# A hybrid decoder step on one core: block transpositions within SBUF, a new layout of two scratch tensors, and the first modulation's weights in tiles of 256 columns

## The chip, the cores and the metric

The kernel runs on one core of a Trainium2 chip. Its metric is device time in microseconds, as the median of several runs. The work is spread over five instruction streams: TensorE (PE, with its weight loads as PEld), VectorE (DVE), ScalarE (ACT), GpSimd (POOL) and SyncE (SP), whose queue issues every DMA of this kernel.

## What is computed

One step of a decoder with two layers, for a prompt of 1024 tokens and 8 samples of one token, which share the weights. Cut from the reference:

```python
cs = jax.nn.silu(c)
for layer in range(DEPTH):                       # 2
    mod = cs @ ada_w[layer] + ada_b[layer]       # (1024 x 3072) weights
    shift, scale, gate = jnp.split(mod[:, None, :], 3, axis=-1)
    h = _rms(x, norm_w[layer]) * (1.0 + scale) + shift
    # layer 0: gated DeltaNet heads (8) and mLSTM heads (8)
    # layer 1: GLA heads (4) and retention heads (4)
    y, states = mixer(h, ...)                    # h @ w_in, the heads, silu gate, @ w_out
    x = x + gate * y
return _rms(x, final_norm_w), states
```

The chunked gated delta rule solves, for each head and each chunk of 128 tokens, a unit lower triangular system `(A + I) U = rhs`.

## The kernel before

**Activations** stand with channels in the partitions and the 1032 tokens (1024 of the prompt, 8 samples) along the free side. Input and output projections are TensorE matmuls in which each factor is split into a high and a low half; weights come in tiles of 512 KB, 1024 rows by 128 columns, are split by ScalarE and VectorE (`halves`), and one projection of 128 columns is 72 matmuls of 344 tokens.

**The order** of all instructions is not that of the program text. The class `Recorder` collects every operation with what it reads and writes (`add`, `touch`), estimates its cost, and plans forward and backward passes over all of them; then `emit` writes each engine's instructions in the planned order. So all instructions of the trace have the line of `emit`, L448, and groups are told apart by tiles. For a DMA, the planner counts 0.36 us on SP's queue, then 0.45 us, its bytes by a rate that follows the shortest run, and 1.4 us to landing, or 2.1 us over 256 KB. For a scratch tensor in DRAM, `region` takes the range from the first to the last element of an access as what it touches, and two accesses whose ranges overlap, one of them a write, are planned one after the other. SP carries out its list in order: a DMA that waits holds up those behind it. Every engine is in order in that sense.

**The start.** `program` loads x, turns it (`turn_x`), takes the root mean squares by token (`rms_tokens`), and normalizes x into eight tiles `xr` (s_aT, s_Y, s_mq, s_mk, s_va, s_kwe, s_qs, s_mp in the trace). Then four groups g follow. In each, `ada_first` (L665) loads four tiles of the first modulation's weights (shift and scale, 2 x 2 blocks of 128 columns with all 1024 rows), multiplies them with the conditioning vectors `cT`, and sums four row groups of TensorE; `layer_h0` makes two of the eight channel blocks of h, and the gates' and the first projection's matmuls for these blocks follow. In the trace the tiles are the loads from in_ada_w before 50 us, and their matmuls those into bank B.

**`squares`** (L1697) turns channels into tokens. VectorE transposes blocks of 32 x 32 from x to y; then the blocks, grouped by 32 partitions, have to change places between partition groups. This is done by DMA: y is written to one of four scratch tensors td in DRAM, 128 rows of 4 KB, and read back in four transfers of 32 partitions, each with four runs of 1 KB per partition. The result is a view of z. Callers are `gdn_mix` (k into s_N, v into s_v; two for each of 8 heads), `mlstm_pair_mix` (s_qs; 4 pairs), `mlstm_mix` (s_pt), `mlstm_out` (s_mp; 8 heads each) and `v_tokens` (s_u, s_v; two for each GLA and each retention head). The written tiles are s_kd, s_vs, s_kwe and s_va.

**`inverse`** (L1279) inverts the triangular system of one gated-delta head. Its diagonal blocks of 32 x 32, for 8 chunks and 4 blocks, are written to the scratch tensor nd in four DMAs, one for each block j, with runs of 128 B. They are read back as 64 blocks of 16 x 16 (`by16`), inverted by 15 steps on VectorE in s_EM, written to the scratch tensor yd and read back by blocks j. The 64 rows of nd and yd are ordered `(c j q)`: chunk, block, half of the block, so that the four blocks j interleave.

In the page, the tensor yd of the output projection's inputs has the same name as the scratch tensor yd of `inverse`; s_EM tells the latter.

Of the kernel before, what the change touches and what calls it, by code (L numbers as in the profile page):

```python
# [9 lines left out]
F32 = mybir.dt.float32  # L10
# [7 lines left out]
T = 1024  # L18
# [4 lines left out]
KT = 8  # L23
L = 128
NC = T // L
# [438 lines left out]
class Step:  # L464
# [200 lines left out]
    def ada_first(self, g, load):  # L665

        nc, a, V = self.nc, self.a, self.nc.vector
        acc = self.ps("B")
        for x in range(4):
            w = load().rearrange("p (k c) -> p k c", k=KT)  # L670
            c0 = 1024 * (x // 2) + 128 * (2 * g + x % 2)
            with self.urgent():
                nc.sync.dma_start(w, a["ada_w"][0, :, c0:c0 + 128].rearrange("(k p) c -> p k c", p=128))
                for k in range(KT):
                    j = k % 4
                    self.mm(acc[32 * j:32 * j + 32, 128 * x:128 * x + 128], self.cT[:, k, :], w[:, k, :],
                            start=k < 4, stop=k >= 4, tile_position=(0, 32 * j))
        with self.urgent():
            sb = self.slot("qg", name="adasb")
            self.act(sb[:, 0:512], acc, AF.Copy)  # L680
            pt = self.ps("B")
            for x in range(4):
                self.tr(pt[:, 128 * x:128 * x + 128], sb[:, 128 * x:128 * x + 128])
            red = sb[:, 512:548].rearrange("p (x c) -> p x c", x=4)
            V.tensor_reduce(red, pt.rearrange("p (x j c) -> p x c j", x=4, j=4)[:, :, 0:9, :], axis=AX.X, op=ALU.add)
            k = slice(2 * g, 2 * g + 2)
            out = self.mod[0][:, 0:16].rearrange("p (s k) c -> p s k c", s=2)[:, :, k]
            o = self.vo["ada_b"]
            bias = self.vec[:, o:o + 16].rearrange("p (s k) -> p s k", s=2)[:, :, k]
            V.tensor_tensor(out, red.rearrange("p (s k) c -> p s k c", s=2),  # L690
                            bias.unsqueeze(3).to_broadcast([128, 2, 2, 9]), op=ALU.add)
            n = self.vo["norm_w"] + 2 * g
            V.scalar_tensor_tensor(self.am[0][:, k], out[:, 1], 1.0,
                                   self.vec[:, n:n + 2].unsqueeze(2).to_broadcast([128, 2, 9]),
                                   op0=ALU.add, op1=ALU.mult)
# [583 lines left out]
    def inverse(self, N):  # L1279

        V, G, dma = self.nc.vector, self.nc.gpsimd, self.nc.sync.dma_start

        nd, yd = (self.nyd[x][self.turn(x, 2)] for x in ("nd", "yd"))
        by32 = lambda x, j: x.rearrange("(c j q) x -> c j (q x)", c=NC, j=4)[:, j, 0:1024].rearrange(
            "c (s t) -> s c t", t=32)
        by16 = lambda x: x[:, 0:512].rearrange("m (r t) -> m r t", t=32)[:, :, 0:16]
        blocks = [slice(32 * j, 32 * j + 32) for j in range(4)]
        t = self.slot("EM", name="inv")
        D, At, qt, Dt = (t[:, 256 * i:256 * i + 256].rearrange("p (c t) -> p c t", c=NC) for i in range(4))
        nb, yb, tb = (t[0:64, 256 * i:256 * i + 256].rearrange("p (r t) -> p r t", t=16) for i in (1, 2, 3))  # L1290
        dma(yb, self.a["i16"].rearrange("p (r t) -> p r t", t=16))
        for j, b in enumerate(blocks):
            dma(by32(nd, j), N[b, :, b])
        dma(nb, by16(nd))
        for s in range(15):
            n = 15 - s
            V.tensor_tensor(tb[:, 0:s + 1, 0:n], yb[:, 0:s + 1, s:s + 1].to_broadcast([64, s + 1, n]),
                            nb[:, s:s + 1, s + 1:16].to_broadcast([64, s + 1, n]), op=ALU.mult)
            V.tensor_tensor(yb[:, 0:s + 1, s + 1:16], yb[:, 0:s + 1, s + 1:16], tb[:, 0:s + 1, 0:n], op=ALU.subtract)
        dma(by16(yd), yb)  # L1300

        for j, b in enumerate(blocks):
            dma(D[b], by32(yd, j))
        V.transpose(Dt, D)
        p = self.ps(None, [128, NC, 32])
        for c in range(NC):
            for j, b in enumerate(blocks):
                self.mm(p[b, c, :], N[b, c, b], Dt[b, c, :], tile_position=(32 * j, 32 * j))
        V.tensor_tensor(At, p, self.imask.unsqueeze(1).to_broadcast([128, NC, 32]), op=ALU.mult)
        p = self.ps(None, [128, NC, 32])  # L1310
        for c in range(NC):
            for j, b in enumerate(blocks):
                self.mm(p[b, c, :], At[b, c, :], D[b, c, :], tile_position=(32 * j, 32 * j))
        V.tensor_tensor(D, D, p, op=ALU.subtract)
        V.transpose(Dt, D)
        Y = self.slot("Y", [128, NC, L], name="Y")
        G.memset(Y, 0.0)
        for b in blocks:
            V.tensor_copy(Y[b, :, b], D[b])

        p = self.ps(None, [128, 2, NC, 32])
        for c in range(NC):
            for i in (0, 2):
                j = i + 1
                bi, bj = slice(32 * i, 32 * i + 32), slice(32 * j, 32 * j + 32)
                self.mm(p[bj, 0, c, :], N[bi, c, bj], Dt[bi, c, :], tile_position=(32 * i, 32 * j))
        for j in (1, 3):
            bj = slice(32 * j, 32 * j + 32)
            self.act(qt[bj], p[bj, 0], AF.Copy, scale=-1.0)
        p2 = self.ps(None, [128, NC, 64])  # L1330
        for c in range(NC):
            for i in (0, 2):
                j = i + 1
                bi, bj = slice(32 * i, 32 * i + 32), slice(32 * j, 32 * j + 32)
                self.mm(p2[bi, c, 0:32], qt[bj, c, :], D[bj, c, :], tile_position=(32 * j, 32 * i))
            self.mm(p2[32:64, c, 0:32], D[32:64, c, :], qt[32:64, c, :], tile_position=(32, 32))
        V.tensor_copy(Y[0:32, :, 32:64], p2[0:32, :, 0:32])
        V.tensor_copy(Y[64:96, :, 96:128], p2[64:96, :, 0:32])

        iy = t[:, 0:512].rearrange("p (c t) -> p c t", c=NC)  # L1340
        Yt = iy[0:64]
        G.memset(Yt[0:32, :, 32:64], 0.0)
        G.tensor_copy(Yt[0:32, :, 0:32], Dt[0:32])
        G.tensor_copy(Yt[32:64, :, 32:64], Dt[32:64])
        V.tensor_copy(Yt[32:64, :, 0:32], p2[32:64, :, 0:32])
        p3 = self.ps(None, [128, NC, 64])
        for c in range(NC):
            self.mm(p3[64:128, c, :], N[0:64, c, 64:128], Yt[:, c, :], tile_position=(0, 64))
        q3 = iy
        self.act(q3[64:128], p3[64:128], AF.Copy, scale=-1.0)  # L1350
        p4 = self.ps(None, [128, NC, 64])
        for c in range(NC):
            self.mm(p4[0:64, c, :], q3[64:128, c, :], Y[64:128, c, 64:128], tile_position=(64, 0))
        V.tensor_copy(Y[0:64, :, 64:128], p4[0:64])
        return Y
# [341 lines left out]
    def squares(self, y, x, z):  # L1697


        dma = self.nc.sync.dma_start  # L1700
        y, z = y[:, 0:T], z[:, 0:T]
        self.nc.vector.transpose(y.rearrange("p (b c j) -> p b c j", b=4, c=NC),
                                 x[:, 0:T].rearrange("p (c b i) -> p b c i", b=4, c=NC))
        d = self.td[self.turn("td", 4)]
        dma(d, y)
        for b in range(4):
            dma(z[32 * b:32 * b + 32].rearrange("i (a x) -> i a x", a=4),
                d.rearrange("(a i) (b x) -> b i a x", a=4, b=4)[b])
        return z.rearrange("p (a c j) -> p c a j", a=4, c=NC)

    def v_tokens(self, v):
# [407 lines left out]
    def build(self):  # L2119
        tc, nc = self.tc, self.nc  # L2120
        with ExitStack() as ctx:
            cp = ctx.enter_context(tc.tile_pool(name="cp", bufs=1))
            psum = ctx.enter_context(tc.tile_pool(name="psum", bufs=1, space=PSUM))
            dr = ctx.enter_context(tc.tile_pool(name="dr", bufs=1, space=DRAM))
# [17 lines left out]
            self.sd = [dr.tile([16, 128], F32, name=f"sd{i}") for i in range(2)]  # L2142
            self.spd = dr.tile([16, W], F32, name="spd")
            self.rd = [dr.tile([4, QB], F32, name=f"rd{i}") for i in range(2)]
            self.td = [dr.tile([128, T], F32, name=f"td{i}") for i in range(4)]
            self.nyd = {x: [dr.tile([64, 528], F32, name=f"{x}{i}") for i in range(2)] for x in ("nd", "yd")}
            self.program()
            with tc.manual_schedule():
# [104 lines left out]
```

## Time and profile before

| | us |
|---|---|
| median of 3 runs | 2255.21 |
| lowest, highest | 2254.8, 2257.08 |
| the profiled execution, its own time | 2262.98 |
| the profiled execution, its span | 2261.2 |
| granted TensorE clock, mean | 0.983 |

The span runs from the first to the last instruction. In the page's second part the span is cut into 40 slices of 56.5 us, with the busy share of each engine in tenths, and the DMA engines' below:

```profile
PE   6999999999999998998989999999999999999998
DVE  6775656576565756666553355745754754755322
DMA  9465564625172535527383222254253253365212
```

TensorE is busy nearly throughout but for the first slice; a busy PE is not PE at its peak. The start lasts to about 100 us, the even layer's heads to about 1195 us; its output projection, the odd layer and the last projection take the rest. In the timeline each row has its start and its length in us, the engine (SPq for the DMAs that SP issues), the operation, what is written and what is read, the count, and in brackets the engine's idle time before it and what ended it.

### The profile page before, as it was taken

Reading aid. Unit: us, or ns where it says so; the run is one execution under the profiler, and the core shown is the slowest. Engines: PE = TensorE matmul, PEld = TensorE weight load, DVE = VectorE, ACT = ScalarE, POOL = GpSimd, SP = SyncE. Lnnn points to the kernel's source line nnn. Section 1 sums busy time; section 2 is a strip of 40 time slices with the busy share of each in tenths; the row PEclk is TensorE's granted clock in tenths of the full one; section 3 lists DMA queues with packets and bytes.
Section 4 is the critical chain, followed back from the end, with each engine's and each line's share of the span. In section 5 each row is a group of like instructions: output and inputs, shape, how many; then the busy total and the mean of one; then the engine's idle time right before and its main releaser. Section 6 shows DMA issues by size and latency. Waiting matters only on the chain.

```text
span 2261.2 us, 42497 instructions
## 1 busy us (share of the span) xinstructions
PE 2184.1 (97%) x17532; PEld 2036.4 (90%) x17532; DVE 1312.8 (58%) x2559; ACT 761.4 (34%) x1374; POOL 588.4 (26%) x409
## 2 busy tenths in 40 slices
PE   6999999999999998998989999999999999999998
PEld 4877877999999988998889999999999999999997
DVE  6775656576565756666553355745754754755322
ACT  4432313242323323232341135234335334334322
POOL 3120212121121311202330032623622622634210
PEclk9999989999999999999999999999999999999999
DMA  9465564625172535527383222254253253365212
GB/s 263 134 190 161 138 190 115 177 78 149 48 189 75 160 99 123 137 77 189 100 253 117 74 80 69 73 153 124 76 157 119 76 162 106 110 192 176 81 59 92
DMA packets 323383, 290.61 MB, mean 129 GB/s; under 512 B 51963, under 2 KB 289013, under 8 KB 323182
## 3 DMA queue, kind: packets, MB, share of 16 engines
q1 hardware_dynamic: 323190, 287.91, 45.2%
q8 instruction: 137, 2.24, 0.4%
q14 instruction: 56, 0.46, 0.1%
HBM read 213.61 MB, written 74.44 MB: 127 GB/s over the span
## 4 chain that ended last, share of the span: by engine, by line
PE 81%; DMA 8%; DVE 6%; ACT 2%; issue 2%; SPq 1%; POOL 0%; POOLq 0%; ACTq 0%; DVEq 0%
PE pj L448 63%; PE A L448 12%; PE B L448 5%; SPq L448 1%; DMA wf<-in_ada_w 1%; DMA s_mp<-td 1%; DVE s_pt L448 1%; DVE wlo L448 1%; DMA s_h<-in_x_prompt 1%; DVE s_tmp L448 1%; DVE arena L448 1%; DMA td<-s_va 1%; DMA s_pt<-yd 0%; DMA td<-s_vs 0%; DMA s_pt<-td 0%
## 5 line engine op out<-in xcount | busy, mean ns | idle before, releaser
L448 PE MATMUL pj<-s_h,whi 128*128 128x344 f32 (+1 forms) x6024 | 1500.0, 328 | 3.7 <-DVE s_h L448 2.6
L448 PEld LDWEIGHTS pj<-s_h,whi 128*128 128x128 f32 (+1 forms) x6024 | 1046.5, 190 | 33.2 <-issue 19.8
L448 PE MATMUL pj<-s_h,wlo 128*128 128x344 f32 (+1 forms) x3024 | 985.2, 326 | 1.0 <-POOL s_h L448 0.6
L448 PEld LDWEIGHTS pj<-s_h,wlo 128*128 128x128 f32 (+1 forms) x3024 | 573.2, 190 | 12.1 <-issue 8.2
L448 ACT ACTIVATE whi<-wf 128x1024 fp32r<-128x1024 f32 (+1 forms) x146 | 152.1, 1042 | 355.1 <-PE pj L448 309.4
L448 DVE TENSOR_TENSOR wlo<-wf,whi 128x1024 fp32r<-128x1024 f32 x112 | 153.3, 1369 | 195.5 <-ACT whi L448 190.9
L448 ACT ACTIVATE s_pt<-pj 128x344 f32<-128x344 f32 (+1 forms) x170 | 76.7, 452 | 237.0 <-PE pj L448 232.4
L448 POOL TENSOR_TENSOR arena<-arena,base 128x8 f32<-128x8 f32 (+5 forms) x38 | 62.2, 1638 | 286.2 <-DVE arena L448 286.2
L448 POOL TENSOR_TENSOR wlo<-wf,whi 128x1024 fp32r<-128x1024 f32 (+1 forms) x32 | 77.4, 2419 | 169.0 <-ACT whi L448 163.5
L448 POOL TENSOR_TENSOR s_tmp<-s_EM 128x512 f32<-128x512 f32 (+1 forms) x60 | 81.3, 1368 | 81.7 <-DVE s_N L448 28.5
L448 DVE SCALAR_TENSOR_TENSOR s_pt<-s_u,base,s_pt 128x1024 f32<-128x1024 f32 x72 | 95.3, 1323 | 0.1
L448 ACT ACTIVATE s_u<-pj 128x344 f32<-128x344 f32 x93 | 41.2, 452 | 136.6 <-PE pj L448 86.8
L448 DVE SCALAR_TENSOR_TENSOR arena<-arena,A 128x128 f32<-128x128 f32 (+1 forms) x84 | 32.8, 390 | 92.5 <-PE A L448 92.4
L448 DVE SCALAR_TENSOR_TENSOR s_zz<-s_pt,pj 128x344 f32<-128x344 f32 x96 | 48.7, 507 | 62.8 <-ACT s_pt L448 62.1
L448 POOL TENSOR_TENSOR s_tmp<-s_tmp,arena 128x1024 f32<-128x1024 f32 (+2 forms) x26 | 45.3, 1747 | 83.2 <-PE B L448 34.2
L448 POOL MEMSET s_u<- 128x3 f32 x24 | 2.5, 102 | 243.4 <-DVE s_pt L448 243.4
L448 POOL TENSOR_TENSOR s_kd<-s_kd,s_vs 128x1032 f32<-128x1032 f32 x8 | 20.0, 2506 | 169.2 <-ACT s_vs L448 169.2
L448 ACT ACTIVATE s_tmp<-s_tmp 128x1024 f32<-128x1024 f32 (+1 forms) x44 | 46.1, 1057 | 35.7 <-POOL s_tmp L448 34.1
L448 DVE TENSOR_TENSOR s_EM<-s_EM 64x15 f32<-64x15 f32 (+7 forms) x240 | 49.9, 208 | 14.2 <-DMA s_EM<-nd 9.0
L448 DVE SCALAR_TENSOR_TENSOR arena<-arena,B 64x130 f32<-64x130 f32 (+1 forms) x84 | 31.2, 372 | 44.4 <-PE B L448 43.6
L448 ACT ACTIVATE arena<-A,arena 128x128 f32<-128x128 f32 x64 | 23.5, 367 | 92.9 <-PE A L448 92.7
L448 ACT ACT_TABLE_LOAD x41 | 52.6, 1283 | 5.1 <-DMA s_h<-in_x_prompt 4.3
(639 smaller groups left out, 3550.4 us busy)
## 6 DMA issues: line engine op xcount, KB each, us to landing
wf<-in_ev_w_in SPq DMA_DIRECT2D x64, 512.0 KB
wf<-in_od_w_in SPq DMA_DIRECT2D x48, 512.0 KB
wf<-in_ada_w SPq DMA_DIRECT2D x32, 512.0 KB
s_tmp<-sd SPq DMA_DIRECT2D x24, 512.0 KB
s_pt<-yd SPq DMA_DIRECT2D x16, 516.0 KB
td<-s_kd SPq DMA_DIRECT2D x16, 512.0 KB
td<-s_vs SPq DMA_DIRECT2D x16, 512.0 KB
s_v<-td SPq DMA_DIRECT2D x64, 128.0 KB
```

The costliest lines, as they stand in the source:

```text
L448: op.fn(*[self.placed(x) for x in op.args], **{k: self.placed(x) for k, x in op.kw.items()})
```

## The change

It has three parts.

- `ada_first`: a tile has 512 rows and 256 columns of one of shift and scale, where it had 1024 rows and 128 columns. Its runs in DRAM are 1 KB, where they were 512 B. It is multiplied with four matmuls of 256 columns in place of eight of 128; two tiles are summed in PSUM for 256 columns.
- `inverse`: the rows of nd and yd are laid out as `(j c q)`, so that each block j has a contiguous stretch.
- `squares`: the way through DRAM is replaced by 16 DMAs from SBUF to SBUF, each 32 partitions by 1 KB; the tensors td are gone.

```diff
@@ ada_first
         for x in range(4):
-            w = load().rearrange("p (k c) -> p k c", k=KT)
-            c0 = 1024 * (x // 2) + 128 * (2 * g + x % 2)
+            w = load().rearrange("p (j c) -> p j c", j=4)
+            y, k0 = x // 2, 4 * (x % 2)
+            c0 = 1024 * y + 256 * g
             with self.urgent():
-                nc.sync.dma_start(w, a["ada_w"][0, :, c0:c0 + 128].rearrange("(k p) c -> p k c", p=128))
-                for k in range(KT):
-                    j = k % 4
-                    self.mm(acc[32 * j:32 * j + 32, 128 * x:128 * x + 128], self.cT[:, k, :], w[:, k, :],
-                            start=k < 4, stop=k >= 4, tile_position=(0, 32 * j))
+                nc.sync.dma_start(w, a["ada_w"][0, 128 * k0:128 * k0 + 512, c0:c0 + 256]
+                                  .rearrange("(j p) c -> p j c", p=128))
+                for j in range(4):
+                    self.mm(acc[32 * j:32 * j + 32, 256 * y:256 * y + 256], self.cT[:, k0 + j, :], w[:, j, :],
+                            start=k0 == 0, stop=k0 == 4, tile_position=(0, 32 * j))
@@ inverse
-        by32 = lambda x, j: x.rearrange("(c j q) x -> c j (q x)", c=NC, j=4)[:, j, 0:1024].rearrange(
+        by32 = lambda x, j: x.rearrange("(j c q) x -> j c (q x)", c=NC, j=4)[j, :, 0:1024].rearrange(
             "c (s t) -> s c t", t=32)
@@ squares
-        d = self.td[self.turn("td", 4)]
-        dma(d, y)
-        for b in range(4):
-            dma(z[32 * b:32 * b + 32].rearrange("i (a x) -> i a x", a=4),
-                d.rearrange("(a i) (b x) -> b i a x", a=4, b=4)[b])
+        for a in range(4):
+            for b in range(4):
+                dma(z[32 * b:32 * b + 32, 256 * a:256 * a + 256], y[32 * a:32 * a + 32, 256 * b:256 * b + 256])
@@ Step.build
-            self.td = [dr.tile([128, T], F32, name=f"td{i}") for i in range(4)]
```

## The prediction, made before the changed kernel was run

> **What bounds the kernel now.** I read the page first (span and engines), then the windows by stage, then who TensorE waited for, and last the timeline around its longest waits.
>
> ```profile
> span 2261.2 us, 42497 instructions
> PE 2184.1 (97%) x17532; PEld 2036.4 (90%) x17532; DVE 1312.8 (58%) x2559; ACT 761.4 (34%) x1374; POOL 588.4 (26%) x409
> ```
>
> The windows of the start, the even layer, and the rest (its output projection and the odd layer) (length; then PE, PEld, DVE, ACT, POOL busy; clock; DMA share; GB/s):
>
> ```profile
> 0.00:100.00 100.00, 80.73 (x639) 65.05 (x640) 68.08 (x148) 47.89 (x97) 31.14 (x47) 0.95 0.71 204
> 100.00:1195.00 1095.00, 1051.56 (x8404) 958.35 (x8403) 692.12 (x1541) 332.01 (x662) 223.71 (x167) 0.98 0.52 140
> 1195.00:2261.20 1066.20, 1051.83 (x8493) 1013.01 (x8491) 552.56 (x870) 381.54 (x616) 333.60 (x195) 0.99 0.37 110
> ```
>
> TensorE sets the end, and its work is not changed by this edit. What can be won is its idle time: 19.3 us in the start, 1095 - 1051.56 = 43.4 us in the even layer, 14.4 us after it. The waits of PE from 100 to 1200 us (us in total, times, longest) say for whom it stood still:
>
> ```profile
> PE pj L448 <- DMA wf<-in_ada_w: 10.3, 3, 4.3
> PE A L448 <- DVE arena L448: 8.7, 1, 8.7
> PE B L448 <- ACT s_va L448: 6.0, 2, 5.5
> ```
>
> The second and the third lead back to `squares`. Their stretches of the timeline (start, us taken, idle before and its releaser):
>
> ```profile
> 882.58 0.38 SPq L448 DMA_DIRECT2D td<-s_va  x1
> 886.24 9.03 SPq L448 DMA_DIRECT2D s_mp<-td  x4
> 902.42 0.48 DVE L448 SCALAR_TENSOR_TENSOR s_zz<-s_mp,base,s_zz 128x256 f32<-128x256 f32 x1 [10.16 <-DMA s_mp<-td]
> 905.06 0.38 PE L448 MATMUL A<-base,arena 128*8 128x128 f32 x1 [8.71 <-DVE arena L448]
> ...
> 1053.81 0.81 SPq L448 DMA_DIRECT2D td<-s_va  x1
> 1060.74 1.95 SPq L448 DMA_DIRECT2D s_pt<-td  x4
> 1066.85 1.06 ACT L448 ACTIVATE s_va<-s_pt 128x1024 f32<-128x1024 f32 x1 [5.72 <-DVE s_EM L448]
> 1068.05 0.77 PE L448 MATMUL B<-s_va,s_kwe 128*128 128x130 f32 x2 [5.50 <-ACT s_va L448]
> ```
>
> From the write to DRAM until the data is used pass 902.42 - 882.58 = 19.8 us in one case and 1066.85 - 1053.81 = 13.0 us in the other. VectorE works in order, so the waiting s_zz holds up the small arena operations behind it, and PE waits for those. After each gap the granted clock stands near half:
>
> ```profile
> 905.00:911.00 6.00, 5.94 (x23) 5.94 (x24) 3.99 (x11) 2.43 (x3) 0.00 (x0) 0.55 0.66 168
> 1068.00:1075.00 7.00, 6.95 (x31) 6.68 (x32) 4.17 (x13) 1.20 (x8) 0.00 (x0) 0.56 0.72 159
> ```
>
> That costs a further 6 x 0.45 = 2.7 us and 7 x 0.44 = 3.1 us.
>
> **The change, part by part. First: the tiles of the first modulation.** There are 16 loads of 512 KB before and after; the runs go from 512 B to 1 KB, and eight matmuls of 128 columns become four of 256, the same columns in all (16 records of one tile took 0.64 us).
>
> ```profile
> 10.00:20.00 10.00, 9.35 (x44) 7.59 (x43) 3.00 (x5) 7.25 (x15) 0.00 (x0) 1.00 1.05 324
> 30.00:40.00 10.00, 5.26 (x120) 3.59 (x120) 10.00 (x6) 1.74 (x3) 9.39 (x3) 1.00 1.01 242
> 50.00:60.00 10.00, 9.70 (x107) 6.99 (x107) 10.00 (x24) 4.59 (x13) 5.84 (x8) 0.99 0.45 117
> ...
> 19.71 7.43 SPq L448 DMA_DIRECT2D s_h<-in_ada_w  x4
> 38.24 0.64 PE L448 MATMUL B<-arena,base 128*32 128x128 f32 x16 [1.32 <-DMA arena<-in_ada_w]
> 43.10 0.44 DVE L448 TENSOR_SCALAR s_aT<-s_aT,base 128x344 f32<-128x344 f32 x1
> 44.12 0.66 PE L448 MATMUL A<-s_h,whi 128*128 128x344 f32 x1 [5.24 <-ACT s_h L448]
> ```
>
> A tile is issued every 7.43 / 4 = 1.86 us, held back by full DMA engines (share 1.01). Half as many runs cannot do better than the mixed stretch of 4 KB rows, 524,288 B at 324 GB/s = 1.62 us: at most 16 x 0.24 = 3.8 us of loading, at the least nothing. I cost it at 0, since VectorE hides it: it is busy 10.00 of 10 us in two of these windows, normalizing x, and the first projection matmul at 44.12 waited for ACT s_h, which waited for the VectorE operation at 43.10, not for a tile. The two short waits for arena tiles before it are absorbed in that 5.24 us. If VectorE were not the cover, it would be worth the 3.8 us. Bounds: -3.8 to +1 (a reordered start).
>
> **Second: `squares`.** It runs 52 times by the code: two in each of 8 gated-delta heads, one in each of 4 mLSTM pairs, two in each of 8 mLSTM heads, two in each of 8 odd blocks. Each goes from one write of 512 KB and four reads of 128 KB to sixteen copies of 32 KB within SBUF: 11 issues more, 572 in all, 396 of them in the even layer; one whole landing less. The price of a piece comes from these rows:
>
> ```profile
> 514.80 1.82 SPq L448 DMA_DIRECT2D nd<-s_N  x4
> 41.71 0.63 SPq L448 DMA_DIRECT2D arena<-in_mlstm_gate_b  x2
> 1407.17 0.34 SPq L448 DMA_DIRECT2D td<-s_vs  x1
> 1410.67 2.51 SPq L448 DMA_DIRECT2D s_v<-td  x4
> 1415.71 1.06 ACT L448 ACTIVATE s_vs<-s_v 128x1024 f32<-128x1024 f32 x1 [1.66 <-DMA s_v<-td]
> ```
>
> Issue: 0.315 us (8 rows of 4 B, two in 0.63) to 0.455 us (the 32 KB writes of nd, four in 1.82); I take 0.45, the row of the same size and number of partitions. Landing of the last piece: no row shows an SBUF to SBUF copy. The last of four 128 KB reads was issued at about 1410.67 + 3/4 x 2.51 = 1412.55 and used 3.2 us later; a quarter of the bytes lies between 0 and 3.2, and I take 2.2, nearer to that row. A transposition is then 15 x 0.45 + 2.2 = 9.0 us (4.7 to 10.0). In the quiet odd layer it takes 1415.71 - 1407.17 = 8.5 us now, so nothing is won there, and 14.4 us of PE idle leave little to lose. In the crowded even layer 19.8 and 13.0 us become 9.0, because SP no longer has to come back for the reads past whatever stands between. So the gap of 8.7 us goes with its 2.7 us of slow clock, and 4.0 of the 5.5 us with half of 3.1: 16.9 us. What is late next is the load of weights behind a burst.
>
> The price: SP is held 16 x 0.45 = 7.2 us instead of some 0.34 + 1.95 = 2.3 us (the write at 1407.17, the reads at 1060.74), 36 x 4.9 = 176 us more over 1095 us, and every weight tile, row broadcast and state load queues behind. Its waits for td go in exchange, and part of those for nd (from 100 to 1200 us):
>
> ```profile
> SPq L448 <- DMA td<-s_vs: 20.9, 5, 6.8
> SPq L448 <- DMA nd<-s_N: 13.7, 7, 4.6
> SPq L448 <- DMA td<-s_va: 7.2, 6, 2.2
> ```
>
> New gaps of PE lie between 0 and the 10.3 us that it waited for late in_ada_w loads, once more, plus some clock; I take +8. The order written out by the planner counts 0.36 us for an issue, so a burst is 16 x 0.09 = 1.4 us longer than it thinks.
>
> **Third: the layout of nd and yd.** The four writes of `inverse` get disjoint stretches of DRAM. The planner's ranges overlapped before, so it spaced them by a landing each and put other issues between; on the chip these others stall:
>
> ```profile
> 895.97 4.03 SPq L448 DMA_DIRECT2D nd<-s_N  x3
> 907.55 0.72 SPq L448 DMA_DIRECT2D nd<-s_N  x1
> 912.58 0.65 SPq L448 DMA_DIRECT2D s_EM<-nd  x1
> ```
>
> From first write to read 16.6 us here; four in a row took 1.82 us in the head at 514.80. The chain of a head gets some 5 us shorter, eight times. But no long gap of PE is charged to nd, since projections fill it: between 0 and -8, I take -3.
>
> **Sum** against the profiled execution's 2262.98 us: 0 - 16.9 + 8 - 3 = -12 us, 2251. The median of the three runs is 2255.21, that is 0.9966 of it: 2243 us, -0.5%.
>
> **Rivals.** *A, slower: bursts starve the odd layer.* Its place is where PE has no slack:
>
> ```profile
> 1204.57 122.72 PE pj L448 x780
> 400.26 0.40 SPq L448 DMA_DIRECT2D wf<-in_ev_w_in  x1
> 405.28 1.06 ACT L448 ACTIVATE whi<-wf 128x1024 fp32r<-128x1024 f32 x1 [4.06 <-DMA wf<-in_ev_w_in]
> L448 POOL TENSOR_TENSOR wlo<-wf,whi 128x1024 fp32r<-128x1024 f32 (+1 forms) x32 | 77.4, 2419 | 169.0 <-ACT whi L448 163.5
> ```
>
> A projection is 72 matmuls of 122.72 / 780 = 0.157 us, 11.3 us; its next weights need 5.0 us to land, 1.06 for the high half and 2.4 for the low one, 8.5 us. The slack is 2.8 us; a burst holds SP for 7.2. Where a load stands right behind one, PE stops for up to 4.4 us; at 3.3 us in each of 8 odd blocks that is 26 us, and with -12 the run is at +14: 2277, or 2269 as median. It decides from an issue of 2.8 / 16 = 0.18 us on, if the load is behind the burst at all; against it speaks that the planner sorts single issues by due time and can set the load between them. Chance 0.18.
>
> *B, slower: the new plan falls out worse.* Every instruction is placed anew. Its place is VectorE in the even layer, held in order behind a late transposition as at 902.42: if the two gaps come back elsewhere and one more pair of their size with them, that is 8.7 + 5.5 + 2.7 + 3.1 = 20 us, less 3 for nd: 2280, or 2272 as median. It decides where bursts land later than the 7.4 us that the planner counts for them (15 x 0.36 + 0.45 + 0.13 + 1.4). Chance 0.10.
>
> *C, no difference: small pieces bring nothing.* If 16 pieces need 13 us in traffic, as the five transfers did at 1053.81, the second gap stays and the first shrinks by 19.8 - 13 = 6.8; 6.8 + 3 - 8 = 2 us are left: 2253 as median. The Trainium skill, "DMA: Bandwidth & Descriptors", section "Rules for kernel authors", says so: coalesce many small transfers, since under 64 KB one pays mostly overhead. By that rule the sixteen pieces should lose to five larger transfers. The trace so far agrees in half: a 32 KB write of nd occupies SP (0.455 us) as long as a read of 128 KB does, but four of them overlap. Chance 0.13; with the case that SP's load eats just what the gaps give, 0.20.
>
> *D, a larger gain.* Both gaps go whole (8.7 + 5.5 + 2.7 + 3.1 = 20 us), nd gives its 8 and SP's new load costs nothing: -28, plus two of the three waits for in_ada_w, about -7: -35, 2228, or 2220 as median. Chance 0.16.
>
> **Chances.** Forecast 0.36, D 0.16, C with its neighbour 0.20, A 0.18, B 0.10. About 0.2% (4.5 us) can be told from no change here; so faster 0.52, same 0.20, slower 0.28. The forecast's own range is 2234 to 2250; the range for 8 in 10 runs from 2222 (most of D) to 2269 (A's price).
>
> **What would show it.** Right: no td in the trace; sixteen issues of `squares` about 7 us long; VectorE's 10.16 us wait and PE's 8.71 and 5.50 us gaps gone; four nd writes in one row; PE idle in the even layer some 10 us lower; PE's first projection matmul still near 44 us, after VectorE. Wrong: that matmul some 3 us earlier (then tiles, not VectorE, set the start); pieces of 0.3 us or of more than 0.5 us; PE waiting for wf in the odd layer (A); even-layer idle at 43 us or above (B).

## The result: 7.9% slower, and the profile after

The changed kernel takes 2433.32 us (median of 4 runs, 2430.86 to 2440.41) where the kernel before takes 2255.75 beside it: a ratio of 1.079, 95% interval 1.0769 to 1.0811. The forecast was 2243, its range ended at 2269. The profiled execution took 2430.86 us, 167.9 more than that of before. The head of its page:

```profile
span 2428.8 us, 42957 instructions
PE 2221.8 (91%) x17404; PEld 2059.5 (85%) x17404; DVE 1295.7 (53%) x2559; ACT 757.6 (31%) x1374; POOL 585.1 (24%) x409
```

TensorE is idle for 2428.8 - 2221.8 = 207.0 us, before for 77.1: 129.9 us of the loss. The other 37.7 us are in its busy time, for the same products. Where it happens is found by a mark that both kernels have, the last issue of `squares` in the even layer. The rows of s_mp, by tile, before and after (ns of one: least, median, most; then first and last start in us):

```profile
L448 SPq DMA_DIRECT2D s_mp<-td x32: 303/430/7536, 284.8 to 1182.2; - x32
```

```profile
L448 SPq DMA_DIRECT2D s_mp<-s_va x128: 507/589/1571, 267.3 to 1320.4; - x128
```

The mark comes at 1320.4 us in place of 1182.2, so 138.2 us are lost in the even layer and 29.4 behind it. The windows up to the mark and from it on, before and then after (length; PE, PEld, DVE, ACT, POOL busy; clock; DMA share; GB/s):

```profile
100.00:1182.20 1082.20, 1038.76 (x8322) 945.54 (x8321) 687.51 (x1536) 329.88 (x660) 221.28 (x166) 0.98 0.52 139
1182.20:2261.20 1079.00, 1064.63 (x8575) 1025.81 (x8573) 557.17 (x876) 383.67 (x618) 336.02 (x196) 0.99 0.37 111
```

```profile
0.00:100.00 100.00, 79.85 (x500) 60.99 (x501) 68.14 (x148) 46.59 (x96) 30.51 (x47) 0.93 0.65 202
100.00:1320.40 1220.40, 1075.32 (x8395) 977.12 (x8394) 678.41 (x1538) 327.44 (x659) 221.09 (x166) 0.94 0.40 108
1320.40:2428.80 1108.40, 1066.68 (x8513) 1021.39 (x8511) 549.13 (x873) 383.58 (x619) 333.51 (x196) 0.98 0.34 101
```

In the even layer PE's idle time goes from 43.4 us to 145.1, and its busy time from 1038.8 to 1075.3 at a granted clock of 0.94 in place of 0.98. VectorE, ScalarE and GpSimd work no longer than before, and the DMA engines carry less (108 GB/s for 139): none of these is busier, and all wait. Only SP has more to do, as is shown below. PE's waits from 100 to 1320.4 us (us in total, times, longest):

```profile
PE pj L448 <- DMA wf<-in_ada_w: 33.4, 10, 8.2
PE B L448 <- ACT s_va L448: 30.4, 3, 18.4
PE pj L448 <- DVE s_zz L448: 17.3, 5, 5.2
PE A L448 <- DVE s_q L448: 13.7, 3, 6.7
```

The longest is a good place to read. The timeline of SP's queue ahead of it, and the rows of ScalarE and PE that it ends with:

```profile
861.43 1.81 SPq L448 DMA_DIRECT2D s_v<-s_vs  x3
863.34 2.01 SPq L448 DMA_DIRECT2D nd<-s_N  x4
865.39 4.32 SPq L448 DMA_DIRECT2D s_v<-s_vs  x7
869.75 0.65 SPq L448 DMA_DIRECT2D s_EM<-nd  x1
870.45 3.83 SPq L448 DMA_DIRECT2D s_v<-s_vs  x6
874.38 0.53 SPq L448 DMA_DIRECT2D wf<-in_ev_w_in  x1
875.00 11.14 SPq L448 DMA_DIRECT2D s_qs<-s_kwe  x16
...
891.02 2.08 SPq L448 DMA_DIRECT2D s_pt<-s_va  x3
893.16 0.65 SPq L448 DMA_DIRECT2D yd<-s_EM  x1
893.85 8.50 SPq L448 DMA_DIRECT2D s_pt<-s_va  x13
```

```profile
903.95 1.06 ACT L448 ACTIVATE s_va<-s_pt 128x1024 f32<-128x1024 f32 x1 [19.74 <-DMA s_pt<-s_va]
905.11 0.77 PE L448 MATMUL B<-s_va,s_mp 128*128 128x130 f32 x2 [18.41 <-ACT s_va L448]
```

Of the 40.9 us from 861.43 to 902.35 SP spends 31.7 on issuing the pieces of three transpositions, sixteen each, one after the other. The third could begin only when the second was through, since its source s_va is made by VectorE, in order, behind an operation that waited for the second:

```profile
887.60 0.69 DVE L448 TENSOR_TENSOR s_kwe<-s_qs,arena 128x512 f32<-128x512 f32 x1 [4.34 <-DMA s_qs<-s_kwe]
889.20 1.22 DVE L448 STREAM_TRANSPOSE s_va<-s_pt 128x1024 f32<-128x1024 f32 x1
```

ScalarE waits 19.74 us for the third's last piece, and PE 18.41 us for ScalarE. PE's list is written out beforehand: what stands behind that matmul cannot go ahead of it. The clock behind the gap, by windows (the columns as above):

```profile
905.20:911.00 5.80, 5.64 (x143) 4.68 (x143) 2.10 (x6) 0.00 (x0) 0.00 (x0) 0.57 0.68 188
```

The waits for wf are of two kinds. The weights for the matmul at 273.62 us, which waited 3.29 us, were issued at 269.82, behind 19.1 us without a pause in which SP had issued 27 pieces. But the two longest of the ten, 8.17 and 7.92 us, end with loads that took 14.4 and 12.5 us to land (the median is 4.3). Just ahead of each stands a write of 64 values of 4 B, out_s_mm issued at 128.66 us for the load at 129.97, and for the other:

```profile
289.32 0.60 SPq L448 DMA_DIRECT2D out_p_mn<-arena  x1
291.88 5.77 SPq L448 DMA_DIRECT2D wf<-in_ada_w  x1
```

These writes themselves took 9.3 and 8.3 us to land, and all 16 packets of this trace that took more than 4 us start within 7 us of such a write. The kernel before has the same writes; which load comes behind one is a matter of the order. No run was made without them, so that they are the cause is not shown.

A piece holds SP for 0.589 us (median; 0.536 for the first of a burst), with 0.633 from one to the next. The sixteen take 15 x 0.633 = 9.5 us to issue and the last one lands 1.88 us later (median of all 832): 11.4 us. The planner counts 15 x 0.36 + 0.45 + 0.13 + 1.4 = 7.4 us to the landing, and 16 x 0.36 = 5.8 us of SP where 16 x 0.633 = 10.1 pass. All issues of SP together take 861 us, before 454; 507 of them are pieces.

### The profile page after: what moved, and what is told of

Its sections match the earlier page's. It is cut to its first block, busy times and chain, and to the rows that moved or that the text cites. A ratio compares the mean times of both kernels' runs of the same rounds, so it can differ in the third digit from the quotient of the medians.

```text
span 2428.8 us, 42957 instructions
## 1 busy us (share of the span) xinstructions
PE 2221.8 (91%) x17404; PEld 2059.5 (85%) x17404; DVE 1295.7 (53%) x2559; ACT 757.6 (31%) x1374; POOL 585.1 (24%) x409
## 5 line engine op out<-in xcount | busy, mean ns | idle before, releaser
L448 PE MATMUL pj<-s_h,whi 128*128 128x344 f32 (+1 forms) x6024 | 1516.6, 330 | 32.6 <-DVE s_zz L448 19.2
L448 DVE TENSOR_TENSOR wlo<-wf,whi 128x1024 fp32r<-128x1024 f32 x112 | 146.3, 1306 | 214.2 <-ACT whi L448 210.9
L448 PE MATMUL pj<-wf,base 128*32 128x512 f32 x128 | 41.5, 674 | 33.4 <-DMA wf<-in_ada_w 33.4
L448 PE MATMUL B<-s_va,s_mp 128*128 128x130 f32 x128 | 28.0, 309 | 28.6 <-ACT s_va L448 20.4
```

What stands on the lines that cost most here:

```text
L448: op.fn(*[self.placed(x) for x in op.args], **{k: self.placed(x) for k, x in op.kw.items()})
```

## The experiments

Ratios are to the kernel before on the same chip in the same hour, with 95% intervals.

| run | us, median | ratio |
|---|---|---|
| e1, td back | 2264.06 | 1.0016 (0.9997 to 1.0035) |
| e2, pieces alone | 2439.41 | 1.0786 (1.0763 to 1.0809) |
| e3, tiles alone | 2265.24 | 1.0026 (1.0006 to 1.0047) |
| e4, nd and yd alone | 2266.66 | 1.0031 (1.0016 to 1.0045) |
| e5, true price told | 2300.05 | 1.0182 (1.0143 to 1.0222) |
| e6, one copy | 2245.43 | 0.9942 (0.9922 to 0.9962) |
| e7, two runs | 2447.02 | 1.0826 (1.0786 to 1.0866) |
| e8, sixteen reads of td | 2352.04 | 1.0407 (1.0383 to 1.0431) |
| e9, before, true price | 2253.10 | 0.9972 (0.9955 to 0.9988) |
| e10, before, price 0 | 2263.64 | 1.0016 (1.0001 to 1.0031) |
| e11, eight copies | 2268.95 | 1.0040 (1.0021 to 1.0058) |
| e12, before, landing early | 2320.94 | 1.0284 (1.0231 to 1.0337) |
| e13, after, landing true | 2400.56 | 1.0635 (1.0601 to 1.0668) |

### Which of the three parts

The first is the kernel after with the old `squares`, the second the kernel before with the new one:

```diff
-        for a in range(4):
-            for b in range(4):
-                dma(z[32 * b:32 * b + 32, 256 * a:256 * a + 256], y[32 * a:32 * a + 32, 256 * b:256 * b + 256])
+        d = self.td[self.turn("td", 4)]
+        dma(d, y)
+        for b in range(4):
+            dma(z[32 * b:32 * b + 32].rearrange("i (a x) -> i a x", a=4),
+                d.rearrange("(a i) (b x) -> b i a x", a=4, b=4)[b])
```

> The changed kernel with the transpositions through DRAM again, so the new tiles and the new layout of nd and yd alone. Theory 'issue' (a piece of 32 partitions holds SP for 0.59 us plus a gap of 0.04, 16 of them 10.1 us, where the planner counts 16 x 0.36 = 5.8; this is the whole loss): back to 2240 to 2260 us. Rival 'reorder' (any change of the list makes the planner's order fall out worse): still over 2300 us.

> The kernel before with the sixteen copies alone. Theory 'issue': 2415 to 2445 us, PE idle in the even layer about 150 us or more, issues of 0.59 us. Rival 'reorder': the loss is shared with the other two parts, so 2300 to 2400 us.

With td back the loss is gone (1.0016, though 2264 us is just over the expected 2260); with the pieces alone it is there whole (1.0786 beside 1.079). It is all in `squares`. The other two parts by themselves, each one hunk of the change put into the kernel before:

> The kernel before with the new tiles of the first modulation alone. Prediction's term: 0 (-3.8 to +1), so 2251 to 2257 us, with the first projection matmul near 44 us if VectorE sets the start; about 41 us if the tiles' landing sets it. Rival 'reorder': over 2265 us.

> The kernel before with the new layout of nd and yd alone. Prediction's term: -3 (0 to -8), so 2247 to 2256 us; the time from the first nd write to the read of nd falls from about 20 us to 10 or less. Rival 'reorder': over 2265 us.

Each costs 0.3%, which is just more than can be told from nothing. Both times miss the ranges by the prediction's terms and lie just where the rival 'reorder' begins (over 2265 us), but the kernel before took 2260.28 us beside them, so what such a new order costs is some 6 us, not the loss of the whole change. The layout of nd does what it says, though: from the first write of nd to its read the eight heads take 5.7 us in the mean (before 17.5). That chain was simply not what PE waited for.

### What the planner is told

The kernel after, its instructions unchanged but for their order:

```diff
+        op.issue = 640.0 if op.size == 32768 and run >= 1024 else 360.0
...
-                free[q] = t + 360.0
+                free[q] = t + op.issue
```

> The changed kernel, in which the planner counts 0.64 us for the issue of a piece (0.36 before); the instructions are the same, only their order is planned anew. Theory 'wrong plan' (the loss is that SP runs later than the order assumes, and engines in order wait for it): most of the 175 us come back, 2260 to 2310 us. Theory 'occupied SP' (16 x 0.63 = 10.1 us for each of 52 calls, 524 us of SP, cannot be hidden in any order): it stays over 2380 us.

2300 us: the same pieces, holding SP just as long (848 us in all), cost 133 us less when the order knows of it. Its page and PE's waits from 100 to 1250 us:

```profile
span 2297.2 us, 42981 instructions
PE 2193.4 (95%) x17404; PEld 2043.0 (89%) x17404; DVE 1312.2 (57%) x2559; ACT 760.7 (33%) x1374; POOL 592.2 (26%) x409
```

```profile
PE A L449 <- DVE s_EM L449: 16.4, 8, 4.7
PE pj L449 <- DMA wf<-in_ada_w: 7.4, 4, 6.4
```

PE's idle time is 103.8 us in place of 207.0; the waits for wf are back to what they were before the change, and those for s_va have left the head of the list. Some 42 us remain against the kernel before.

### What a piece costs, and why

One copy of all 128 partitions within SBUF (the exchange between the groups is left out), and pieces of two runs of 512 B:

```diff
-        for a in range(4):
-            for b in range(4):
-                dma(z[32 * b:32 * b + 32, 256 * a:256 * a + 256], y[32 * a:32 * a + 32, 256 * b:256 * b + 256])
+        dma(z, y)
```

> The changed kernel with one copy of 128 partitions by 4 KB in place of the sixteen pieces; the exchange of blocks between partition groups is left out, so the values differ. The same bytes, one issue of about 0.35 us, one hop in place of two. Theory 'issue': no loss at all, 2235 to 2260 us, which is also what the missing hop is worth against the kernel with td (2256 to 2264). If the copying within SBUF were slow in itself, it stays over 2300 us.

```diff
-                dma(z[32 * b:32 * b + 32, 256 * a:256 * a + 256], y[32 * a:32 * a + 32, 256 * b:256 * b + 256])
+                dma(z[32 * b:32 * b + 32, 256 * a:256 * a + 256].rearrange("p (u w) -> p u w", u=2),
+                    yb[32 * a:32 * a + 32, b])
```

> The changed kernel with each piece as two runs of 512 B per partition in place of one of 1 KB (VectorE's transposition writes its blocks in two halves for that, two instructions in place of one). Sixteen pieces as before. If the issue time hangs on the pattern (reads of td with four runs per partition took 0.43 us, the pieces with one run 0.59), it falls to 0.43 and the run to 2330 to 2380 us; if it hangs on the 32 partitions, it stays at 0.59 and 2420 to 2445 us.

Then the pieces fetched from DRAM instead of SBUF (td is written once, as before), and eight copies of 64 partitions, each block staying in its group, with the planner told 0.60 us for each:

```diff
+        d = self.td[self.turn("td", 4)]
+        dma(d, y)
         for a in range(4):
             for b in range(4):
-                dma(z[32 * b:32 * b + 32, 256 * a:256 * a + 256], y[32 * a:32 * a + 32, 256 * b:256 * b + 256])
+                dma(z[32 * b:32 * b + 32, 256 * a:256 * a + 256], d[32 * a:32 * a + 32, 256 * b:256 * b + 256])
```

> The kernel after, with the write to td back, and read back in sixteen pieces of 32 partitions by 1 KB from DRAM (the same pieces as the copies within SBUF, and one write more). It tells what makes the piece dear. Theory 1 (the source in SBUF makes it dear): a piece from DRAM takes SP 0.31 to 0.45 us, like the 128 KB reads of td (0.43) or the tiles of 128 partitions (0.34); 16 x 0.40 = 6.4 us, close to the 5.8 that the planner counts, so the plan holds and the time is 2270 to 2300 us. Theory 2 (the shape, 32 partitions of one run, makes it dear): 0.59 us again, SP's issue time near 861 + 52 x 0.34 = 880 us, and 2430 us or more.

```diff
-            for b in range(4):
-                dma(z[32 * b:32 * b + 32, 256 * a:256 * a + 256], y[32 * a:32 * a + 32, 256 * b:256 * b + 256])
+            for b in range(2):
+                dma(z[64 * b:64 * b + 64, 256 * a:256 * a + 256], y[64 * b:64 * b + 64, 256 * a:256 * a + 256])
```

> The kernel after with eight copies of 64 partitions by 1 KB in place of sixteen of 32 (left out: the exchange of blocks between partition groups; each stays where it is), the planner told 0.60 us for each. If the price of an issue goes by the DMA, with little for its partitions: 0.50 to 0.59 us, SP's issue time 354 + 52 x 8 x 0.57 = 590 us. Theory (with a true plan, what remains is SP being held; 2245 us at 352 us of issue time with one copy, 2300 at 848 with sixteen): between, 2265 to 2280 us. Rival (with a true plan a held SP is harmless up to some point, and the last 42 us of the sixteen pieces are the burst's own length): 2245 to 2255 us, as with one copy.

The rows of the tile s_mp or s_pt, in the order one copy, two runs, sixteen reads from DRAM, eight copies:

```profile
L448 SPq DMA_DIRECT2D s_mp<-s_va x8: 477/506/1065, 294.6 to 1167.2; - x8
```

```profile
L448 SPq DMA_DIRECT2D s_mp<-s_va x128: 585/595/1932, 308.1 to 1335.2; - x128
```

```profile
L448 SPq DMA_DIRECT2D s_pt<-td x128: 302/419/1965, 199.2 to 1217.3; - x128
L448 SPq DMA_DIRECT2D td<-s_va x16: 326/360/4873, 191.1 to 1257.9; - x16
```

```profile
L449 SPq DMA_DIRECT2D s_mp<-s_va x64: 461/594/1726, 216.2 to 1197.0; - x64
```

From DRAM the very same piece holds SP for 0.419 us, from SBUF for 0.589: with SBUF as the destination, the source is what makes it dear, not its 32 partitions, nor one run or two. One copy of sixteen times the bytes is cheaper (0.506), though dearer than the write of as much to DRAM (0.360). So theory 1 of the sixteen reads had the cause right, with the price right inside the 0.45 that I had taken; but its time was wrong: 2352 us, not at most 2300. SP is held 17 times, 740 us in all, and as many pieces at a moderate price still cost 4%. This run also keeps the write to td and its landing, which the copies within SBUF don't have, so the 4% are not the price of the pieces alone. The Trainium skill, "DMA: Bandwidth & Descriptors", section "Issuing engines are not separate DMA queues", calls the time that the sequencer takes to initiate a DMA usually small relative to the DMA itself. It is not here: 0.59 of 1.88 us.

The kernels whose order knows the price, or comes within 0.14 us of it, give the worth of SP's time:

| | SP's issues, us | time, us |
|---|---|---|
| one copy (told 0.36 for 0.50) | 352 | 2245.43 |
| before, told 0.46 | 440 | 2253.10 |
| before (told 0.36 for 0.46) | 454 | 2258 to 2260 |
| eight copies, told 0.60 | 592 | 2268.95 |
| sixteen copies, told 0.64 | 848 | 2300.05 |

About 0.1 us of time for each us of SP: 23.5 for 240 from one copy to eight, then 31.1 for 256; the kernel before, told 0.46, lies between (7.7 for 88). The eight copies speak against the length of the burst as the cause: in the even layer their transposition takes 9.9 us from first issue to last landing in the mean, before 12.8, and yet the kernel is slower than before. With that, the last 42 us of the sixteen pieces go best with SP being held; that the pieces on another engine's queue would give them back wasn't tried.

### Which error of the plan costs

The kernel before, all its instructions kept, with the planner told 0.46 us for every issue, or nothing for those of td:

```diff
+        op.issue = 460.0
```

> The kernel before, its instructions unchanged, its planner told 0.46 us for every issue of SP instead of 0.36 (454 us of issue time over 990 DMAs is 0.458). Theory (the error in the planner's price is what costs): a truer plan is a little faster, 2245 to 2255 us against 2258. Rival (plans differ by chance by some 5 us, and only a price that is wrong by hundreds of us in sum matters, as in the kernel after): within 0.3% of before.

```diff
+        op.issue = 0.0 if any(x.name.startswith("td") for x in writes + reads) else 360.0
```

> The kernel before, its instructions unchanged, its planner told 0 us on SP for each DMA that writes or reads td. It underrates a transposition of the kernel before by 1.8 + 0.5 = 2.3 us, 120 us over 52, about half of the 4.3 x 52 = 224 us by which the planner underrates the pieces of the kernel after. Theory (an underrated queue alone, without a single DMA more, costs most of what is underrated: some 135 us for 224): 30 to 80 us slower, 2290 to 2340 us, and the drift between planned and real issue grows through the even layer. Rival (the planner's error does no harm unless SP is really full: before, SP issues for 454 of 2260 us): less than 10 us slower.

A true price makes the kernel before 0.28% faster (0.12 to 0.45); this is the fastest kernel with the whole computation, ahead of both. A price of nothing costs 0.16%, so the theory of that run fell. Part of the reason can be read in the planner's constants: it also counts the bytes one transfer after the other, for a transposition by td 524,288 B at 340 and as many at 260 B per ns, 3.6 us in all, and that bounds its plan whatever an issue costs. For sixteen pieces the bytes take 2.0 us of its time and the issues 5.8, so there the issue decides. This left two candidates, told apart by the landing, first underrated in the kernel before, then mended alone in the kernel after:

```diff
+        op.late = -2050.0 if any(x.name.startswith("td") for x in writes + reads) else 0.0
...
-                end = dma + (2100.0 if op.size > 1 << 18 else 1400.0)
+                end = dma + (2100.0 if op.size > 1 << 18 else 1400.0) + op.late
```

> The kernel before, its instructions unchanged, its planner told that each transfer to and from td lands 2.05 us earlier than it counted: a transposition is underrated by 4.1 us, as the pieces of the kernel after are (it counts 7.4 us from first issue to last landing, the chip takes 15 x 0.633 + 1.9 = 11.4). Theory (what costs in the kernel after is that every chain through a transposition comes 4 us later than the order was made for; the price of SP's time does not matter, as the run before this one with that price at nothing cost 0.2%): PE's order puts the users of the result too early, 36 times in the even layer, up to 36 x 4.1 = 148 us: 2330 to 2400 us. Rival (an underrated landing is absorbed where SP is free, and the loss needs the long bursts): below 2275 us.

```diff
+        op.late = 4100.0 if op.size == 32768 and run >= 1024 else 0.0
```

> The kernel after, its instructions unchanged; the planner still counts 0.36 us of SP for a piece, but the landing of each piece 4.1 us later, so that the last one lands when it really does (11.5 us after the first issue). Theory (the underrated landing alone makes the loss): as with the true price of an issue, 2290 to 2320 us, though SP is still underrated by 4.3 us at each burst. Rival (what counts is that the SP queue is 4.3 us longer per burst than the plan has it, which delays everything behind): 2400 to 2440 us.

An underrated landing, with not a DMA more and SP's issues at 442 us in all, costs 62 us, somewhat less than the 70 that I had as the least. Its window from 100 to 1195 us:

```profile
100.00:1195.00 1095.00, 1015.95 (x8068) 924.19 (x8069) 647.64 (x1500) 309.11 (x628) 208.22 (x159) 0.95 0.46 127
```

PE is idle for 79.1 us there, before for 43.4, and the clock is 0.95 for 0.98: the picture of the kernel after, at a smaller size. But the run does not set late results apart from a held queue. Since the plan counts the write to td as landed too early, SP comes to the reads too early and stands there until it has; what is behind them waits too. The two largest of these waits, from 100 to 1195 us:

```profile
SPq L449 <- DMA td<-s_va: 42.8, 13, 6.9
SPq L449 <- DMA td<-s_vs: 25.6, 7, 6.7
```

With those for s_kd and s_kwe they make 97.4 us, where the kernel before has 38.3. How the 62 us divide between the two is not shown.

The other run has no td, and it shows that the landing is the smaller part of the loss. With the landing of the last piece told right and the price of SP left at 0.36, 2400.56 us: 33 us come back, and 100 more when the price is told too (2300). Its PE waits from 100 to 1250 us:

```profile
PE pj L449 <- DMA wf<-in_ada_w: 29.5, 8, 8.7
PE A L449 <- DVE arena L449: 18.8, 4, 11.3
```

The wait for weights is nearly what it was after (33.4), though the transpositions are no longer late by the plan; with the price told it is 7.4. That speaks for the queue, but it is not a steady sign: with the pieces alone, at the same loss, it is 16.9 us. The times of the two runs carry the argument.

So the 175 us divide, told in this order, into 33 for results that land 4.1 us later than planned, 100 for SP's queue that each burst holds 4.3 us longer than planned, and 42 that stay when the plan knows both.

## Why the prediction was wrong

**What bounds the kernel.** Right: PE's idle time sets it, and its arithmetic did not change. Its waits and the slow clock behind them make the whole loss.

**The tiles: 0.** The cover that was named is the right one. The rows of the first projection after:

```profile
43.18 0.44 DVE L448 TENSOR_SCALAR s_aT<-s_aT,base 128x344 f32<-128x344 f32 x1
44.20 0.66 PE L448 MATMUL A<-s_h,whi 128*128 128x344 f32 x1 [7.41 <-ACT s_h L448]
```

PE starts at 44.20 us (before 44.12, with the tiles alone 43.19), again after ScalarE, which waited for VectorE. By itself this part measured +0.26%, some 6 us, which the bounds of -3.8 to +1 do not hold; the 0.3% of the nd part is of the same size, and what of either is only another order was not tried.

**The layout of nd and yd: -3.** The mechanism was right. The four writes go in a row, and the read follows:

```profile
571.16 1.87 SPq L448 DMA_DIRECT2D nd<-s_N  x4
...
575.21 0.66 SPq L448 DMA_DIRECT2D s_EM<-nd  x1
```

From first write to read the eight heads take 5.6 us in the mean, 12 us less than before; more than the 5 that were reckoned. It gained nothing: alone, the part costs 0.31%. The upper bound of 0 for it was wrong too.

**The piece.** The landing was right (1.88 us for 2.2). The issue was not: 0.45 was taken, with 0.455 as the upper bound, from writes and reads that have DRAM on one side, and no row showed a copy within SBUF. At 0.589, with 0.633 from piece to piece, the burst takes 11.4 us to the landing and not 9.0, and holds SP for 10.1 and not 7.2. The row of the same size and number of partitions was the wrong one, and the bounds were drawn as if the kind of source did not count.

**The price of SP's time: the step that failed.** The prediction put a burst as "1.4 us longer than" the planner "thinks" and laid nothing on it, and +8 us on all that queues behind SP. The runs put 133 us on the first (33 for late landings, 100 for the queue) and some 42 on the second. A burst was 4.3 us longer than planned, not 1.4, but a better price for the piece would hardly have saved the forecast: sixteen pieces from DRAM at about the 0.45 that was taken (0.464 from piece to piece), with the write to td besides, cost 4%.

**The gain of 16.9 us** was not to be had, and its reason was misread. SP did not have to come back for the reads past other issues: by the trace the write to td landed at 886.22 us in the first case and the reads began at 886.24, in the second at 1060.63 and 1060.74. The transfers themselves were late. In the first case two of the reads landed 15 us after their issue, one of them holding SP for 7.54 us, and ahead of them stands again a write of 64 values of 4 B:

```profile
883.85 1.13 SPq L448 DMA_DIRECT2D out_p_mn<-arena  x1
```

It landed after 8.27 us, and all 33 packets of more than 4 us in the trace of before start within 7 us of such a write. Copies within SBUF can come behind one too: in the kernel after, a piece issued at 1163.27 us, after such a write at 1161.32, took 10.2 us to land. A transposition of the even layer, reckoned at 9.0 us, takes 15.3 in the mean from first issue to last landing, where it took 12.8 by td, and the longest gap before a matmul on s_va is 18.41 us where it was 5.50.

**The rivals.** *B* had the mechanism and its condition, bursts that land later than the 7.4 us that the planner counts, and the sign of it came true: even-layer idle over 43 us, 145.1. By the prediction's own sum, 9.0 us against 7.4, this condition was met from the start, and yet *B* had a chance of 0.10. Its price of 20 us was two gaps of the old kind; in fact PE stands still for more than 2 us 26 times in the even layer, before 6 times. *A* did not happen as told. In the rest, from 1320.4 us on, PE waits for VectorE and hardly for weights:

```profile
PE B L448 <- DVE s_aT L448: 8.7, 3, 4.7
PE B L448 <- DVE arena L448: 8.0, 4, 4.1
PE pj L448 <- DVE s_h L448: 6.5, 2, 5.2
```

In all PE is idle for 27 us more than before behind the mark. That this is about the 26 us of *A* is chance, since the waits are others. *C*, by which small pieces bring nothing, points the right way: the sixteen pieces do lose to five larger transfers, and the one large copy beats them all, but by far more than its "no difference". *D* was out of reach at any price of the pieces that was measured.

## What to carry to other kernels

Before one large DMA is cut into many small ones, count the time for which they hold the queue that issues them, from a row with the same kind of source and destination; where there is none, the bound has to be open on the dear side. Where the order of the work is written out by a planner, a new kind of instruction needs its true price in the planner first: here the same instructions took 2433 or 2300 us by that number alone. And a shorter chain is worth nothing as long as nobody waits for its end, as the nd part shows.

## What the hardware showed unexpectedly

- A copy within SBUF holds SP longer than a transfer with DRAM on one side: 0.589 us against 0.419 for the same 32 partitions of 1 KB, 0.506 against 0.360 for 128 partitions of 4 KB. Partitions (32 or 64, 0.589 and 0.594) and runs (one or two, 0.589 and 0.595) hardly change it.
- It lands quickly: 1.88 us after its issue (median), and the same piece from DRAM in 1.90.
- The eight writes of 64 values of 4 B (out_p_mn) in the kernel before take 7.1 to 10.5 us to land, and transfers issued right behind one were seen to take up to 15 us.
